# A hybrid mLSTM and DeltaNet block on one core: the order of the wide output blocks, the loads of the last stage, the values' factors, and the queue of the heads' turned outputs

## The chip, the cores and the metric

The kernel runs on one core of one Trainium2 chip. The metric is the device time of one execution in microseconds, as the median of several runs; lower is better.

## The reference, cut to what matters

S = 512 tokens, D = 2048 channels, float32, one layer: RMSNorm, one input projection that is cut into two token mixers and their gates, and one output projection whose halves are merged by gates and added to the residual.

```python
u = _rmsnorm(h, norm_w)
proj = jnp.matmul(u, w_in)                # ml q,k,v,o,z,i,f; dn qkv,z,b,a; gate_a, gate_b
...
h_a = _mlstm_chunkwise(q, k, v, i_pre, logf)          # 8 heads, 128 / 256 wide
h_a = _merge_heads(_rmsnorm(h_a)) * ml_norm_w * sigmoid(ml_o) * silu(ml_z)
...
qkv = _causal_conv_silu(dn_qkv, dn_conv_w)            # 4 taps
h_b = _gated_delta_chunkwise(l2norm(q), l2norm(k), v, beta, g)   # 16 heads, 128 wide
h_b = _merge_heads(_rmsnorm(h_b) * dn_norm_w * silu(dn_z))
...
# delta rule, chunk by chunk, after a triangular solve for w_val and w_k:
u = wv - wk @ S;  o = qd @ S + qk_c @ u;  S_new = ge * S + ke.T @ u
...
y_a, y_b = h_a @ w_out[:ML_WIDTH], h_b @ w_out[ML_WIDTH:]
out = rmsnorm(h + sigmoid(gate_a) * y_a + sigmoid(gate_b) * y_b)
```

## The kernel before, in words

Each float32 operand of a large product is split into a high part (a cast on ACT, line 135, `wh`) and a low part (a subtraction on DVE, line 138, `wl`), and each product is three matmuls of 128 x 128 by 128 x 512: high by high, low by high, high by low.

The program has these stages. First RMSNorm and the first projections, to about 24 us and a little beyond. Then a long row of stages `seven`, which make the projections for gates and values with seven products instead of eight (to about 1062 us). Then the mixers (1062 to 1835 us): eight units `dn_unit`, each with two DeltaNet heads, amid the projections `proj_cm` of the next units (PE's lines 261 to 263, product `pj`) and the mLSTM heads. Then the output projection: three blocks of 512 columns by `wide_block` (blocks 0 and 1 for the mLSTM half, and block 2 over the DeltaNet half, 1940 to 1996 us), two stages `seven`, and a last block.

A unit of the mixers runs `dn_front_k` and `dn_front_q` and then `dn_back`, which inverts the triangular blocks of both heads in four steps (PE products `p1` to `p4`, with copies into `ta` and `tb` between them) and starts two chains `dn_chain`, one for each head. A chain's first product is `pw`, line 1006, which takes `tb` and the values `vn` (tile `vt`). The values must have been multiplied by the keys' norms `nk` (line 980). At its end a chain makes the squares' sums `ssq` (line 1034), and multiplies its accumulator `po` by the gate `gz` (line 1040): with that the accumulator's bank is free. `turn` then transposes the result on DVE (line 796, tile `to`), and `travel` sends it in four DMAs of 64 KB each to `h_d` in memory (line 806). mLSTM heads go to `hm_d` in the same way.

`wide_block` has four accumulators `ps`, one for 128 tokens each (chunk c), in banks of three pools: `psj` (that of the projections), `psw` (small work) and `pso` (the chains' accumulators). A step is one row block kt of the weights: for c = 0 to 3 three matmuls (lines 1315 to 1317), with a tick after c = 1 and after c = 3. The last KTAIL steps are done chunk by chunk, each followed by `put_y(c)` (line 1338). Blocks 0 and 1 start while the last unit still works; `close()` looks after every step whether pools can be given back, and with the last starts `h_last`.

Block 2 takes DeltaNet's hidden rows. `load_h2` loads 16 tiles `hr`, in turn from `he_d` and `h_d`, through four buffers, and splits each into `uh` and `ul` (line 1189). `he_d` holds half-sums that `h_sums` and, for the last two heads, `h_last` make (`hsum`, lines 1248 to 1251, scaled into `tu`) and write. `h_last` waits five ticks, then loads the last two heads into two of the same four buffers. `lead` prepares the stage after block 2: three `load_quad` of three loads each (line 505). The gates of block 2 are loaded into the tile X (line 1330).

The order of work: PE runs in the order in which the program is written. For the other engines a scheduler orders the instructions by simulated time and priority. `tick()` moves the program's clock by one step, once every six matmuls, and lets generators go on that were given to `start(gen, wait)`; `yield n` waits n ticks. `urgent(level)` raises the priority. `behind(e)` places an instruction on engine e's queue right behind the newest split or weight load there, instead of where its priority would take it. `newest["S"]` is the newest weight load on SyncE's queue (SP).

Of the kernel before, what the change touches and what calls it, by code (L numbers as in the profile page):

```python
# [55 lines left out]
def hybrid_body(  # L56
# [83 lines left out]
    def behind(eng):  # L140

        return tc.issue_after(newest[eng])
# [102 lines left out]
    psw = pss.enter_context(tc.tile_pool(name="psw", bufs=3, space=PSUM))  # L245
    pso = pss.enter_context(tc.tile_pool(name="pso", bufs=2, space=PSUM))

    banks = (((psj, "pj"),) * 3 + ((psw, "wk"),), ((psw, "wk"),) * 2 + ((pso, "o"),) * 2)

    def proj_cm(col0, before=None, kind="i"):  # L250
        ps = [psj.tile([P, S], F32, tag="pj", name="pj") for _ in range(2)]
# [232 lines left out]
    def seven_stage(sbp, su, s4, X, t2_d, w_, k0, blocks, sinks, hook):  # L484
# [5 lines left out]
                 for g in "AB" for i in range(KH)]  # L490
        rawq, partq = [], {}

        def load_quad():
            if len(rawq) == len(quads):
                return
            _, c1, c2, b, g, i = quads[len(rawq)]
            with tc.high_priority(offset=2 * PRIO):
                r = sbp.tile([P, 3, NO], F32, tag="wr3", name="wr3", bufs=3)
                k1, k2 = (slice((k0 + 2 * i + n) * P, (k0 + 2 * i + n + 1) * P) for n in range(2))
                if g == "A":  # L500
                    src = (w_[k1, c1:c1 + NO], w_[k1, c2:c2 + NO], w_[k2, c2:c2 + NO])
                else:
                    src = (w_[k2, c1:c1 + NO], w_[k2, c2:c2 + NO], t2_d[b % 2, i])
                for n in range(3):
                    nc.sync.dma_start(r[:, n, :], src[n])  # L505
            rawq.append(r)

        def split(src, wide):
            if wide:
# [92 lines left out]
                    hook()  # L602
                product(n, m)

        def lead():
            for _ in range(3):
                load_quad()
                yield 2
            prep_sums(0)
            prep_pair(0)  # L610
            yield 1
# [151 lines left out]
    def bc(col, n):  # L763
        return col.unsqueeze(2).to_broadcast([P, NC, n])

    def conv_silu(ps, ct, dst, level=1):
        yp = yps[cnt["yp"] % NYP]
        cnt["yp"] += 1
        with urgent(level):
            A.copy(yp[:, 3:S + 3], ps)  # L770
            A.mul(dst, yp[:, 3:S + 3], convc[:, 144 + ct:145 + ct])
# [27 lines left out]
    def travel(o, dst, out, apart):  # L799

        d = dst if len(dst.shape) == 4 else dr.tile([16, BS, 4, BS], F32, tag="td", name="td", bufs=8)
        ov = o.rearrange("p n (j c) -> p (n j) c", c=BS)
        if out:
            for a in range(4):
                with behind("A"):
                    nc.scalar.dma_start(d[:, :, a, :].rearrange("m r c -> r m c"), ov[a * BS:(a + 1) * BS])
# [124 lines left out]
    def dn_back(hs, kq, u):  # L931
# [15 lines left out]
        for q in range(2):  # L947
            a1 = slice(64 * q + 32, 64 * q + 64)
            with urgent():
                A.mul(s1[a1], p1[a1], -1.0)  # L950
        yield 2
        p2 = psw.tile([P, 2, 2 * NC, BS], F32, tag="wk", name="p2")
        for g, a in G2:
# [20 lines left out]
            T.matmul(p4[0:64, g, :], s3[64:128, g, :], tb[64:128, g, 64:128], start=True, stop=True)  # L974
        with urgent():
            V.tensor_copy(tb[0:64, :, 64:128], p4[0:64])
        for j in range(2):
            vn = u["vs"][j]
            with behind("V"):
                V.tensor_tensor(out=vn, in0=vn, in1=bc(u["nk"][:, j, :], P), op=ALU.mult)  # L980
        start(dn_chain(0, hs, kq, u), 2)
        start(dn_chain(1, hs, kq, u), 3)

    def dn_chain(j, hs, kq, u):
        h = hs[j]
# [57 lines left out]
    def dn_unit(p, mh):  # L1043
# [28 lines left out]
            start(load_h(), 2, "B")  # L1072
        ps = proj_cm(DN_Q + dcol)
        u["qn"] = []
        for j in range(2):
            conv_silu(ps[j], hs[j], kq[j][:, 1, :], 3 if last else 1)
            qn = wp.tile([P, NC, P], F32, tag="tg", name="qn", bufs=3)
            u["qn"].append(qn)
            start(silu_end(kq[j][:, 1, :], (kq[j][:, 1, :], qn)), 4 + 3 * j, front)
# [148 lines left out]

    def h_raw(i):
        if i == KH - 1:  # L1230
            raw = [late["sb"].tile([P, S], F32, tag="hs", name="hs", bufs=4) for _ in range(2)]
        elif i % 2:
            raw = [wk.tile([P, S], F32, tag="rb", name="hs", bufs=3) for _ in range(2)]
        else:
            pair = wk.tile([P, 2, S], F32, tag="ls", name="hs", bufs=1)
            raw = [pair[:, n, :] for n in range(2)]
        with behind("S"):
            for n in range(2):
                load_tile(raw[n], h_d[2 * i + n])
        return raw  # L1240
# [29 lines left out]

    def h_last():

        yield 5
        raw = h_raw(KH - 1)
        yield 5
        yield from h_pair(KH - 1, raw)
# [42 lines left out]
    def wide_w(col, kt):  # L1319
        return [w[:, 0, :] for w in next_w("o", col, kt)]  # L1320

    def wide_block(nb, pools, place, then=()):

        sl = slice(nb * NO, (nb + 1) * NO)
        ps = [pool.tile([P, NO], F32, tag=t, name="py") for pool, t in pools]
        tgs = {}

        def load_tg(c):
            tgs[c] = place(c)
            nc.sync.dma_start(tgs[c], tg_d[c, :, sl])  # L1330

        def load_tgs():
            for c in range(NC - (nb == 1)):
                load_tg(c)
            yield 1

        def put_y(c):
            V.scalar_tensor_tensor(out=tgs[c], in0=tgs[c], scalar=1.0, in1=ps[c], op0=ALU.add, op1=ALU.mult)
# [12 lines left out]
        for kt in ks[:KT - KTAIL]:  # L1351
            w = wide_w(nb * NO, kt)
            for c in range(NC):
                products(ps, kt, c, *w, ks)
                if c % 2:
                    tick()
            if nb < YDRAIN:
                close()
        ws = [(kt, wide_w(nb * NO, kt)) for kt in ks[KT - KTAIL:]]
        for c in range(NC):  # L1360
            for kt, w in ws:
                products(ps, kt, c, *w, ks)
            tick()
            if c in tgs:
                with urgent(3):
                    put_y(c)
            else:
                start(put_last(), 1)
# [2 lines left out]
             wk.tile([P, NO], F32, tag="rb", name="tgy", bufs=3) if c == 2 else wp.tile([P, NO], F32, tag="tg", name="tgy", bufs=3),  # L1371
             lambda c: wp.tile([P, NO], F32, tag="tg", name="tgy", bufs=3))
    for b in range(YDRAIN):
        wide_block(b, ((psj, "pj"), (psw, "wk"), (psj, "pj"), (psj, "pj")), DRAIN[b])
    while "sb" not in late:
        tick()
        close()
# [278 lines left out]
```

## Time and profile before

| | |
|---|---|
| median of 3 runs | 2220.33 us (2218.37 to 2221.66) |
| the profiled execution | 2217.53 us |
| its span, first to last instruction | 2215.8 us |
| mean granted TensorE clock | 0.995 |
| mixers | 1062.7 to 1835.0 us |
| blocks 0 and 1 | 1835.0 to 1940.7 us |
| block 2 | 1940.7 to 1996 us |

How to read the lines below: a row of a timeline has the start in us, the duration, engine, line, operation, output <- inputs and the shape; in square brackets the idle time of the engine before it and what ended it. A row of the waits has the engine and line that waited, what ended the wait, the total in us, how often, and the longest. A row of the DMAs has the transfer, the queue that issued it, how many, KB each, and the median us from issue to landing. SPq is SyncE's queue, ACTq that of ScalarE.

### The profile page before, as it was taken

How to read it: one execution, taken by the hardware profiler on the slowest of the kernel's cores; microseconds unless marked ns; L12 is line 12 of the kernel's file. 1: busy time of each engine (PE TensorE's matmuls, PEld its weight loads, DVE VectorE, ACT ScalarE, POOL GpSimd, SP SyncE). 2: the span in 40 equal slices, each digit the busy share in tenths (PEclk: the TensorE clock that was granted, in tenths of full speed). 3: DMA queues.
4: the chain of work that ended last, by engine and by line, in shares of the span. 5: the costliest groups of instructions: out<-in, count | busy, mean ns of one | idle time of the engine just before them, and what ended most of it. 6: DMA issues, size and time to landing. Idle time of an engine off the chain costs nothing.

```text
span 2215.8 us, 31667 instructions
## 1 busy us (share of the span) xinstructions
PE 2156.6 (97%) x10592; PEld 1770.1 (80%) x10592; DVE 1655.4 (75%) x2883; ACT 1022.3 (46%) x1986; POOL 279.5 (13%) x388
## 2 busy tenths in 40 slices
PE   6999999999999999999999999999999999989997
PEld 5877778887878888888888888888888887867775
DVE  5787788788778777777587886757575777667875
ACT  5444444444444444444545545444545464334344
POOL 0320000000000000000223323213131211110101
PEclk9999999999999999999999999999999999999999
DMA  5455676667677766766677767667666668696896
GB/s 157 119 182 180 197 214 198 210 197 223 199 217 238 227 192 225 233 229 213 190 195 165 184 161 182 161 171 174 167 154 153 154 166 221 176 265 189 249 326 215
DMA packets 532774, 435.81 MB, mean 197 GB/s; under 512 B 241921, under 2 KB 393698, under 8 KB 532482
## 3 DMA queue, kind: packets, MB, share of 16 engines
q1 hardware_dynamic: 420450, 349.29, 55.3%
q10 hardware_dynamic: 105568, 68.77, 9.8%
q0 software_dynamic: 6592, 15.73, 3.7%
q8 instruction: 83, 1.36, 0.3%
q14 instruction: 81, 0.66, 0.1%
HBM read 342.37 MB, written 95.49 MB: 198 GB/s over the span
## 4 chain that ended last, share of the span: by engine, by line
PE 71%; DMA 12%; DVE 9%; issue 4%; ACT 2%; SPq 2%; POOL 1%; ACTq 0%; DVEq 0%; POOLq 0%
PE ps L576 10%; PE ps L577 10%; PE ps L575 10%; PE pj L261 9%; PE pj L263 9%; PE pj L262 9%; DVE wl L138 4%; DMA wr<-t_d 4%; DMA wr<-in_w_in_dram 2%; PE py L1315 2%; PE py L1316 2%; PE py L1317 2%; ACT wh L135 1%; SPq L505 1%; DVE X L617 1%
## 5 line engine op out<-in xcount | busy, mean ns | idle before, releaser
L135 ACT CAST wh<-wr 128x512 fp32r<-128x512 f32 (+1 forms) x538 | 379.6, 707 | 411.3 <-PE pj L262 225.0
L138 DVE TENSOR_TENSOR wl<-wr,wh 128x512 fp32r<-128x512 f32 (+1 forms) x538 | 440.9, 822 | 154.8 <-ACT wh L135 150.5
L261 PE MATMUL pj<-uh,wh 128*128 128x512 f32 x1024 | 427.2, 417 | 0.0
L263 PE MATMUL pj<-uh,wl 128*128 128x512 f32 x1024 | 401.1, 392 | 0.0
L262 PE MATMUL pj<-ul,wh 128*128 128x512 f32 x1024 | 400.5, 391 | 0.0
L576 PE MATMUL ps<-wl,uh 128*128 128x512 f32 x704 | 277.1, 394 | 7.4 <-DVE wl L138 7.2
L575 PE MATMUL ps<-wh,uh 128*128 128x512 f32 x704 | 276.1, 392 | 4.4 <-DVE X L617 3.9
L577 PE MATMUL ps<-wh,ul 128*128 128x512 f32 x704 | 274.3, 390 | 0.0
L135 ACT CAST wh<-ts 128x512 fp32r<-128x512 f32 x224 | 138.2, 617 | 256.0 <-DVE ts L535 200.2
L135 ACT CAST wh<-t 128x1024 fp32r<-128x1024 f32 x112 | 117.8, 1052 | 248.6 <-PE ps L577 133.1
L263 PEld LDWEIGHTS pj<-uh,wl 128*128 128x128 f32 x1024 | 192.5, 188 | 42.3
L576 PE MATMUL ps<-wl,suh 128*128 128x512 f32 x576 | 224.2, 389 | 1.7 <-DVE wl L138 1.7
L575 PE MATMUL ps<-wh,suh 128*128 128x512 f32 x576 | 224.3, 389 | 0.6 <-ACT qk L353 0.3
L577 PE MATMUL ps<-wh,sul 128*128 128x512 f32 x576 | 224.1, 389 | 0.0
L261 PEld LDWEIGHTS pj<-uh,wh 128*128 128x128 f32 x1024 | 193.4, 189 | 34.9
L262 PEld LDWEIGHTS pj<-ul,wh 128*128 128x128 f32 x1024 | 193.5, 189 | 32.9
L138 DVE TENSOR_TENSOR wl<-ts,wh 128x512 fp32r<-128x512 f32 x224 | 153.6, 689 | 38.6 <-ACT wh L135 38.6
L138 DVE TENSOR_TENSOR wl<-t,wh 128x1024 fp32r<-128x1024 f32 x112 | 137.7, 1229 | 48.3 <-ACT wh L135 47.6
L576 PEld LDWEIGHTS ps<-wl,uh 128*128 128x128 f32 x704 | 132.2, 188 | 44.1 <-DVE wl L138 18.3
L575 PEld LDWEIGHTS ps<-wh,uh 128*128 128x128 f32 x704 | 132.1, 188 | 39.2 <-DVE X L617 11.3
L535 DVE TENSOR_TENSOR ts<-wr 128x512 f32<-128x512 f32 x112 | 77.3, 690 | 102.0 <-DMA wr<-t_d 76.1
L577 PEld LDWEIGHTS ps<-wh,ul 128*128 128x128 f32 x704 | 132.2, 188 | 26.4
(305 smaller groups left out, 3499.8 us busy)
## 6 DMA issues: line engine op xcount, KB each, us to landing
wr<-in_w_in_dram SPq DMA_DIRECT2D x704, 256.0 KB, 3.7
wr<-in_w_out_dram SPq DMA_DIRECT2D x138, 256.0 KB, 5.0
t_d<-ts ACTq DMA_DIRECT2D x96, 256.0 KB, 4.2
wr<-t_d SPq DMA_DIRECT2D x96, 256.0 KB, 4.0
wr<-in_w_in_dram SPq DMA_DIRECT2D x64, 128.0 KB, 3.3
xt<-in_x_dram SPq DMA_DIRECT2D x8, 512.0 KB, 7.3
tg_d<-X ACTq DMA_DIRECT2D x16, 256.0 KB, 5.5
tg_d<-to ACTq DMA_DIRECT2D x16, 256.0 KB, 5.0
```

The costliest lines, as they stand in the source:

```text
L135: newest["A"] = A.copy(hi, src).ins
L138: newest["V"] = V.tensor_tensor(out=lo, in0=src, in1=hi.bitcast(F32), op=ALU.subtract).ins
L261: T.matmul(ps[j], hi[:, k, wsl], uh[:, kt, :], start=(kt == 0), stop=False)
L262: T.matmul(ps[j], hi[:, k, wsl], ul[:, kt, :], start=False, stop=False)
L263: T.matmul(ps[j], lo[:, k, wsl], uh[:, kt, :], start=False, stop=(kt == KT - 1))
L535: V.tensor_tensor(out=ts[:, 0, :], in0=r[:, 0, :], in1=r[:, 2, :], op=ALU.subtract)
L575: T.matmul(ps[t], ah, hi, start=(g == "A" and i == 0), stop=False, skip_group_check=True)
L576: T.matmul(ps[t], ah, lo, start=False, stop=False, skip_group_check=True)
L577: T.matmul(ps[t], al, hi, start=False, stop=(i == KH - 1), skip_group_check=True)
L1315: T.matmul(ps[c], uh[:, kt, tsl], hi, start=(kt == ks[0]), stop=False)
L1316: T.matmul(ps[c], uh[:, kt, tsl], lo, start=False, stop=False)
L1317: T.matmul(ps[c], ul[:, kt, tsl], hi, start=False, stop=(kt == ks[-1]))
```

## The change

It has six parts. Line numbers of the kernel after are 8 to 17 higher.

1. `wide_block` takes `behind_` and `ending`. In block 0 (`behind_` = 2) the first two steps are done for chunks 0 and 1, and then for chunks 2 and 3; in block 2 the last steps end in the order of chunks 2, 0, 1, 3. Block 2's banks are (psw, psw, pso, psj) instead of (psw, psw, pso, pso).
2. `lead` for the stage after block 2 issues its nine loads one a tick behind the newest weight load, starting at tick 14 instead of three quads at raised priority from tick 18.
3. In `dn_back` the multiplications of the values by the norms come after the first step instead of after the fourth, and the chains start one tick later.
4. `travel` issues the DMAs of `h_d` and `hm_d` from SP's queue, behind the newest weight load, instead of from ACT's.
5. In the last unit the copies of both heads' last projection (`conv_in`) are written ahead of the filters.
6. `h_last` loads into the tile X, which is still empty then, and without its first wait.

```diff
-    banks = (((psj, "pj"),) * 3 + ((psw, "wk"),), ((psw, "wk"),) * 2 + ((pso, "o"),) * 2)
+    JB, WB, OB = (psj, "pj"), (psw, "wk"), (pso, "o")
...
-        def lead():
+        def lead(apart=False):
             for _ in range(3):
-                load_quad()
-                yield 2
+                if apart:
+                    for to, src in quad_parts():
+                        with behind("S"):
+                            nc.sync.dma_start(to, src)
+                        yield 1
+                else:
+                    load_quad()
+                    yield 2
...
-    def conv_silu(ps, ct, dst, level=1):
+    def conv_in(ps, level=1):
         yp = yps[cnt["yp"] % NYP]
         cnt["yp"] += 1
         with urgent(level):
             A.copy(yp[:, 3:S + 3], ps)
+        return yp
...
-                with behind("A"):
-                    nc.scalar.dma_start(d[:, :, a, :].rearrange("m r c -> r m c"), ov[a * BS:(a + 1) * BS])
+                with behind("S"):
+                    nc.sync.dma_start(d[:, :, a, :].rearrange("m r c -> r m c"), ov[a * BS:(a + 1) * BS])
...
                 A.mul(s1[a1], p1[a1], -1.0)
+        for j in range(2):
+            vn = u["vs"][j]
+            with behind("V"):
+                V.tensor_tensor(out=vn, in0=vn, in1=bc(u["nk"][:, j, :], P), op=ALU.mult)
         yield 2
...
             V.tensor_copy(tb[0:64, :, 64:128], p4[0:64])
-        for j in range(2):
-            vn = u["vs"][j]
-            with behind("V"):
-                V.tensor_tensor(out=vn, in0=vn, in1=bc(u["nk"][:, j, :], P), op=ALU.mult)
-        start(dn_chain(0, hs, kq, u), 2)
-        start(dn_chain(1, hs, kq, u), 3)
+        start(dn_chain(0, hs, kq, u), 3)
+        start(dn_chain(1, hs, kq, u), 4)
...
+        yq = [conv_in(ps[j], 3) for j in range(2)] if last else (None, None)
         for j in range(2):
-            conv_silu(ps[j], hs[j], kq[j][:, 1, :], 3 if last else 1)
+            conv_silu(ps[j], hs[j], kq[j][:, 1, :], yp=yq[j])
...
         if i == KH - 1:
-            raw = [late["sb"].tile([P, S], F32, tag="hs", name="hs", bufs=4) for _ in range(2)]
+            raw = [late["X"][:, 0, n, :] for n in range(2)]
...
     def h_last():
 
-        yield 5
         raw = h_raw(KH - 1)
...
-        for kt in ks[:KT - KTAIL]:
-            w = wide_w(nb * NO, kt)
-            for c in range(NC):
-                products(ps, kt, c, *w, ks)
-                if c % 2:
-                    tick()
-            if nb < YDRAIN:
+        ws = {}
+        order = [(kt, c) for c in (0, 2) for kt in range(behind_) ] + [(kt, c) for kt in ks[behind_:KT - KTAIL] for c in (0, 2)]
+        for n, (kt, c0) in enumerate(order):
+            if c0 == 0:
+                ws[kt] = wide_w(nb * NO, kt)
+            for c in (c0, c0 + 1):
+                products(ps, kt, c, *ws[kt], ks)
+            tick()
+            if n % 2 and nb < YDRAIN:
                 close()
         ws = [(kt, wide_w(nb * NO, kt)) for kt in ks[KT - KTAIL:]]
-        for c in range(NC):
+        for c in ending:
...
-        wide_block(b, ((psj, "pj"), (psw, "wk"), (psj, "pj"), (psj, "pj")), DRAIN[b])
+        wide_block(b, (JB, WB, JB, JB), DRAIN[b], behind_=0 if b else 2)
...
-    wide_block(YDRAIN, banks[1], lambda c: X2[:, c // 2, c % 2, :], [(load_h2(), 1), (lead(), 18)])
+    wide_block(YDRAIN, (WB, WB, OB, JB), lambda c: X2[:, c // 2, c % 2, :], [(load_h2(), 1), (lead(True), 14)], ending=(2, 0, 1, 3))
```

Three places show how the instructions move. On ACT at the start of block 0, where the last unit's copies of a projection (`yp` <- `pj`) free two of the block's banks, there stands before (`kq` are the filters' outputs, `hr` the hidden rows of the mLSTM half):

```order
L1189 ACTIVATE uh<-hr,normc 128x512 x2
L135 CAST wh<-wr 128x512
L806 DMA h_d<-to 32x16x32 x3
L770 COPY yp_9097<-pj 128x512
L806 DMA h_d<-to 32x16x32
L771 ACTIVATE kq_17041<-yp_9097,convc 128x512
L770 COPY yp_9099<-pj 128x512
L135 CAST wh<-wr 128x512
L806 DMA h_d<-to 32x16x32 x2
L771 ACTIVATE kq_17042<-yp_9099,convc 128x512
```

and after:

```order
L135 CAST wh<-wr 128x512
L1205 ACTIVATE uh<-hr,normc 128x512
L779 COPY yp_9097<-pj 128x512
L1205 ACTIVATE uh<-hr,normc 128x512
L786 ACTIVATE kq_17041<-yp_9097,convc 128x512
L135 CAST wh<-wr 128x512
L1205 ACTIVATE uh<-hr,normc 128x512
L779 COPY yp_9099<-pj 128x512
L786 ACTIVATE kq_17042<-yp_9099,convc 128x512
```

The six issues of `h_d` have left ACT's row, and two scalings of hidden rows and a cast now stand between the two copies, where one multiplication stood.

On DVE at the end of block 1 and the head of block 2, where the last unit's two chains end (`gz` <- `po` frees a chain's bank), there stands before:

```order
L1034 SCALAR_TENSOR_TENSOR ssq<-ssq,qe 128x4
L1040 TENSOR_TENSOR gz<-po,gz 128x512
L1338 SCALAR_TENSOR_TENSOR tgy<-tgy,py 128x512
L796 STREAM_TRANSPOSE to<-gz 128x512
L1338 SCALAR_TENSOR_TENSOR tgy<-tgy,py 128x512
L138 TENSOR_TENSOR wl<-wr,wh 128x512
L1248 TENSOR_TENSOR hsum<-hs 128x256
L1250 TENSOR_TENSOR hsum<-hs 128x256
L1190 SCALAR_TENSOR_TENSOR tu<-hsum,normc,tu 128x768
L1040 TENSOR_TENSOR gz<-po,gz 128x512
```

and after:

```order
L1049 SCALAR_TENSOR_TENSOR ssq<-ssq,qe 128x4 x2
L1353 SCALAR_TENSOR_TENSOR tgy<-tgy,py 128x512 x2
L138 TENSOR_TENSOR wl<-wr,wh 128x512
L1264 TENSOR_TENSOR hsum<-hs 128x256
L1266 TENSOR_TENSOR hsum<-hs 128x256
L138 TENSOR_TENSOR wl<-wr,wh 128x512
L1265 TENSOR_TENSOR hsum<-hsum,hs 128x256
L1206 SCALAR_TENSOR_TENSOR tu<-hsum,normc,tu 128x768
L1055 TENSOR_TENSOR gz<-po,gz 128x512
```

The first chain's multiplication has moved behind the second's sum of squares, two outputs of block 1, two weight splits, three sums and a scaling; the second chain's follows two rows below.

On SP, the queue of loads in block 2, the last gates of block 1 (`tgy`) are followed before by:

```order
L1330 DMA tgy<-tg_d 128x512
L176 DMA wr<-in_w_out_dram 128x512 x4
L505 DMA wr_19285<-in_w_out_dram 128x512 x3
L176 DMA wr<-in_w_out_dram 128x512
L505 DMA wr_19311<-in_w_out_dram 128x512 x3
L505 DMA wr_19337<-in_w_out_dram 128x512
L176 DMA wr<-in_w_out_dram 128x512
L505 DMA wr_19337<-in_w_out_dram 128x512 x2
L1289 DMA hr<-he_d 128x512
L1186 DMA hr<-h_d 128x4x128
```

and after by:

```order
L1345 DMA tgy<-tg_d 128x512
L176 DMA wr<-in_w_out_dram 128x512 x2
L821 DMA h_d<-to 32x16x32 x5
L176 DMA wr<-in_w_out_dram 128x512
L821 DMA h_d<-to 32x16x32 x3
L1202 DMA X_19056<-h_d 128x4x128
L176 DMA wr<-in_w_out_dram 128x512
L1202 DMA X_19056<-h_d 128x4x128
L1304 DMA hr<-he_d 128x512
L1202 DMA hr<-h_d 128x4x128
```

The nine loads of the last stage (`wr_...`, line 505) no longer stand ahead of the first hidden rows `hr`; the two heads' outputs and the loads of them into X stand there instead, with weight loads between and behind them.

In `dn_back` the two multiplications (line 980, now 969) stood before the copy into `tb` (line 976) in DVE's row, two rows ahead in most units; after, they stand 11 to 23 rows ahead of it (line 995).

More of the change, by code (lines that the diff above doesn't have):

```diff
@@ L491, in seven_stage, with quad_parts @@
         rawq, partq = [], {}
+        def quad_parts():
+            _, c1, c2, b, g, i = quads[len(rawq)]
+            r = sbp.tile([P, 3, NO], F32, tag="wr3", name="wr3", bufs=3)
+            k1, k2 = (slice((k0 + 2 * i + n) * P, (k0 + 2 * i + n + 1) * P) for n in range(2))
+            if g == "A":
+                src = (w_[k1, c1:c1 + NO], w_[k1, c2:c2 + NO], w_[k2, c2:c2 + NO])
+            else:
+                src = (w_[k2, c1:c1 + NO], w_[k2, c2:c2 + NO], t2_d[b % 2, i])
+            rawq.append(r)
+            return [(r[:, n, :], src[n]) for n in range(3)]
         def load_quad():
@@ L495, in load_quad @@
                 return
-            _, c1, c2, b, g, i = quads[len(rawq)]
             with tc.high_priority(offset=2 * PRIO):
[L498 to L506, printed above, removed]
+                for to, src in quad_parts():
+                    nc.sync.dma_start(to, src)
         def split(src, wide):
@@ L603, in seven @@
                 product(n, m)
-        def lead():
+        def lead(apart=False):
             for _ in range(3):
-                load_quad()
-                yield 2
+                if apart:
+                    for to, src in quad_parts():
+                        with behind("S"):
+                            nc.sync.dma_start(to, src)
+                        yield 1
+                else:
+                    load_quad()
+                    yield 2
             prep_sums(0)
@@ L770, in conv_silu @@
             A.copy(yp[:, 3:S + 3], ps)
+        return yp
+    def conv_silu(ps, ct, dst, level=1, yp=None):
+        if yp is None:
+            yp = conv_in(ps, level)
+        with urgent(level):
             A.mul(dst, yp[:, 3:S + 3], convc[:, 144 + ct:145 + ct])
@@ L1320, in wide_w, with wide_block @@
         return [w[:, 0, :] for w in next_w("o", col, kt)]
-    def wide_block(nb, pools, place, then=()):
+    def wide_block(nb, pools, place, then=(), behind_=0, ending=range(NC)):
         sl = slice(nb * NO, (nb + 1) * NO)
```

## The prediction

> **What bounds the kernel now.** I read the page's busy times first, then the waits of TensorE (PE) over the whole run, then PE's timeline at those of them that the change touches, with the granted clock behind each.
>
> ```profile
> PE 2156.6 (97%) x10592; PEld 1770.1 (80%) x10592; DVE 1655.4 (75%) x2883; ACT 1022.3 (46%) x1986; POOL 279.5 (13%) x388
> PE pw L1006 <- DVE tb L976: 4.0, 4, 1.9
> PE py L1315 <- ACT wh L135: 5.9, 3, 4.1
> PE py L1315 <- ACT yp L770: 2.1, 2, 1.8
> PE py L1315 <- DVE gz L1040: 1.9, 1, 1.9
> PE ps L575 <- DVE X L1338: 1.6, 1, 1.6
> ```
>
> TensorE is busy for 97% of 2215.8 us, and the change removes none of its matmuls. So only two things can be gained: its idle time, and matmuls run at less than the full clock. In the rows of the waits the columns are the total in us, the times and the longest. The five rows touch lines that the change moves: 4.0 + 5.9 + 2.1 + 1.9 + 1.6 = 15.5 us. Where they stand:
>
> ```profile
> 1676.95 0.49 PE L1006 MATMUL pw<-vt,tb 128*128 128x128 f32 x2 [1.90 <-DVE tb L976]
> 1838.31 0.50 PE L1315 MATMUL py<-wh,uh 128*128 128x512 f32 x1 [1.77 <-ACT yp L770]
> 1942.12 0.39 PE L1315 MATMUL py<-wh,uh 128*128 128x512 f32 x1
> 1942.57 0.39 PE L1317 MATMUL py<-wh,ul 128*128 128x512 f32 x1
> 1944.87 0.47 PE L1315 MATMUL py<-wh,uh 128*128 128x512 f32 x1 [1.92 <-DVE gz L1040]
> 1988.46 0.80 PE L1315 MATMUL py<-wh,uh 128*128 128x512 f32 x1 [4.14 <-ACT wh L135]
> 1998.37 0.50 PE L575 MATMUL ps<-wh,tu 128*128 128x512 f32 x1 [1.60 <-DVE X L1338]
> ```
>
> Behind some of them the clock falls. The columns of the windows are busy time by engine, then PEclk, the granted clock:
>
> ```profile
> 1677.00:1680.40 3.40, 3.40 (x18) 2.88 (x19) 3.40 (x6) 2.65 (x12) 0.00 (x0) 1.00 0.28 73
> 1839.82:1843.23 3.41, 3.41 (x9) 2.64 (x10) 3.41 (x9) 2.86 (x6) 0.00 (x0) 0.50 1.20 311
> 1945.64:1949.04 3.40, 3.40 (x9) 2.64 (x8) 2.48 (x5) 0.90 (x2) 0.00 (x0) 0.50 0.99 221
> 1988.46:1993.42 4.96, 4.87 (x11) 3.50 (x12) 3.79 (x7) 2.17 (x3) 0.60 (x1) 0.50 0.80 249
> ```
>
> At clock 0.50 half of the stretch is lost: 3.41 / 2 = 1.7 us after block 0's wait, 1.7 us at the head of block 2, 4.96 / 2 = 2.5 us at its end. After the wait of 1.90 us in the mixers nothing is lost (1.00). Of the row of 5.9 I count only the longest wait, 4.1. So the ceiling of the gain is 4.0 + (2.1 + 1.7) + (1.9 + 1.7) + (4.1 + 2.5) + 1.6 = 19.6 us.
>
> The Trainium skill's "TensorE: Matmul & The Clock Gate", section "What's actually happening", lets the array fall to half rate after an idle window of about 3.4 us. The trace differs: 1.77 and 1.92 us of idling were enough at two places, and 1.90 us at a third was not. By the rule only the 4.14 us wait would carry a clock loss, and the ceiling would be lower by 3.4 us; the rows decide.
>
> **The change part by part.** All durations are from the profiled execution: 2217.53 us, 2215.8 of span and 1.7 around it, against a median of 2220.33. A saving is taken off either alike.
>
> *The values' factors (dn_back).* In DVE's timeline two multiplications by the norms stand ahead of the copy for which `pw` waits:
>
> ```profile
> 1673.57 1.29 DVE L980 TENSOR_TENSOR vt<-vt,nk 128x512 f32<-128x512 f32 x2
> 1676.22 0.68 DVE L976 COPY tb<-p 64x512 f32<-64x512 f32 x1
> ```
>
> The copy comes 1.29 us sooner without them, and the chains start one tick later, six matmuls at (1942.57 − 1942.12) / 2 = 0.23 us, 1.4 us. Together 2.7 us of room against a longest wait of 1.90: all four go, **−4.0** (0 if the filters' operations in line 773 take the place; no more than −4.0, as the clock shows no loss here). The multiplications themselves now stand among filter work three program steps sooner; DVE is busy for 75%, and the steps between wait two or three ticks each, 2.7 to 4.1 us, so 1.3 us there is hidden. Should that cover be gone, the four waits come back one step sooner.
>
> *Block 0's order and the last unit's copies.* Chunks 2 and 3 of block 0 need banks that ACT's copies of the last projection free.
>
> ```profile
> 1837.67 0.59 ACT L770 COPY yp<-pj 128x512 f32<-128x512 f32 x1 [0.94 <-DVE wl L138]
> 1838.40 0.72 ACT L771 ACTIVATE kq<-yp,convc 128x512 f32<-128x512 f32 x1
> 1839.03 0.56 ACT L770 COPY yp<-pj 128x512 f32<-128x512 f32 x1
> 1839.49 0.62 ACT L135 CAST wh<-wr 128x512 fp32r<-128x512 f32 x1
> ```
>
> Now: 2.1 of idling and 1.7 of clock, 3.8 us. After, chunk 2 is wanted six matmuls (1.4 us) later, and ACT has no outputs to issue, whose place was in the 0.94 us of idling. But as the instructions stand now, two scalings of hidden rows, a multiplication and a cast lie between the two copies: 0.59 + 0.72 × 3 + 0.62 = 3.4 us from copy to copy, where it was 1839.03 − 1837.67 = 1.36 us. Copy 1 would end near 1837.67 + 3.4 + 0.56 = 1841.6, less the 0.94; chunk 3 is wanted at 1838.31 − 1.77 + 1.4 + 0.7 = 1838.6. That is about 2 us of waiting again: **0** (−3.8 if the scalings' loads come late and the copies pass first; +2 if the 0.94 isn't saved and the clock falls longer).
>
> *Block 2's banks.* Its chunk 3 waited for chain 1's accumulator, read by L1040; now chunk 3 has a bank that has long been free, and chunk 2 has chain 0's.
>
> ```profile
> 1943.12 1.00 DVE L1190 SCALAR_TENSOR_TENSOR tu<-hsum,normc,tu 128x768 fp32r<-128x768 f32 x1
> 1944.05 0.68 DVE L1040 TENSOR_TENSOR gz<-po,gz 128x512 f32<-128x512 f32 x1
> ```
>
> Before, chain 0's reader stood well ahead of this; in the new order on DVE it is behind both norms' sums, two more outputs of block 1, two weight splits, three sums and this `tu`, where chain 1's stood. So it ends near 1944.05 + 0.68 = 1944.7, while chunk 2 is wanted at 1942.12 (the row of PE above): 2.6 us instead of 1.92, and the same clock loss. **+0.5** (−3.6 if chain 0 stays ahead; +2.5 if the chain's later tick and the larger gap add up).
>
> *Block 2's end.* Its last weight cast came late because ACT takes it behind scalings that wait for loads, and SP had issued nine loads for the final stage ahead of those:
>
> ```profile
> 1957.68 1.28 SPq L505 DMA_DIRECT2D wr<-in_w_out_dram  x3
> 1964.20 0.33 SPq L1289 DMA_DIRECT2D hr<-he_d  x1
> 1987.18 0.72 ACT L1189 ACTIVATE uh<-hr,normc 128x512 fp32r<-128x512 f32 x1 [0.88 <-DMA hr<-h_d]
> 1987.81 0.60 ACT L135 CAST wh<-wr 128x512 fp32r<-128x512 f32 x1
> ```
>
> Now 4.14 + 2.5 = 6.6 us. After, the first loads of hidden rows pass the nine, which come one a tick, and h_last's two tiles take none of the four buffers those use. A new chain stands in SP's queue instead. L1040 of chain 1 ends near 1946; the transposes end near 1947.5; the issues and landings:
>
> ```profile
> L806 ACTq DMA_DIRECT2D h_d<-to x64: 309/443/2421, 1242.8 to 1951.8; - x64
> DMA to landing us min/median/max: 2.4/3.9/8.3
> hs<-h_d SPq DMA_DIRECT2D x2, 256.0 KB, 6.1
> he_d<-hs ACTq DMA_DIRECT2D x2, 256.0 KB, 5.0
> wr<-in_w_out_dram SPq DMA_DIRECT2D x19, 256.0 KB, 5.7
> X<-tg_d SPq DMA_DIRECT2D x4, 256.0 KB, 5.7
> ```
>
> Four issues of 0.44 make 1949.3, landing 3.9 makes 1953.2, the load of them 6.1 (1959.3), sums and scaling an estimated 3.5 (1962.8; the scaling alone is the 1.00 of `tu`), the sum written 5.0 (1967.8), and only then may X take its gates; a weight load behind their issues leaves at about 1969.2. Block 2 starts at 1940.7 (six matmuls ahead of 1942.12) and a step is 12 × 0.23 = 2.76 us, so its twelfth is used at 1940.7 + 11 × 2.76 + 3.6 (head) = 1974.7, and its load must leave at 1974.7 − 5.7 − 0.6 (cast) − 0.7 (split, an estimate from the cast) = 1967.7: 1.5 us late. So I keep 1.5 of the 6.6: **−5.1** (−6.6 to +3; more in the third rival).
>
> *The order of its end.* With chunk 2 and chunk 0 first, the final stage's first banks are read early: **−1.6** (to 0).
>
> *The outputs' queue.* 128 issues leave ACT for SP. In the mixers:
>
> ```profile
> SPq L176 <- DVE wl L138: 128.0, 69, 6.1
> td<-ke SPq DMA_DIRECT2D x8, 64.0 KB, 2.4
> wr<-in_w_in_dram SPq DMA_DIRECT2D x2, 256.0 KB, 2.8
> wr<-in_w_in_dram SPq DMA_DIRECT2D x186, 256.0 KB, 3.0
> L261 PE MATMUL pj<-uh,wh 128*128 128x512 f32 x1024 | 427.2, 417 | 0.0
> ```
>
> SP waits 128 us there for weight buffers to come free, so it is early; a head's four issues, 4 × 0.44 = 1.8 us, fit into that. A weight load issued amid 64 KB pieces (the third row, in a window of 9 us with eight such pieces) landed in 2.8 us against 3.0 for all 186, and no projection waits for its weights (0.0 in the last row). I take 0 in the mixers and **+0.7** for block 2, where outputs stand ahead of weights (0 to +6).
>
> The Trainium skill's "DMA: Bandwidth & Descriptors", section "Issuing engines are not separate DMA queues", says that issuing from several engines saves only the sequencer's time of starting the DMA. By it the 1.8 us a head would be the whole price; no run so far shows the outputs on SP.
>
> Sum: −4.0 + 0 + 0.5 − 5.1 − 1.6 + 0.7 = −9.5. The profiled execution would become 2208.0, the median 2210.8: **2211**. A measurement of this kernel can tell about 0.2%, 4.4 us, from no change.
>
> **The rivals.**
>
> *All of it goes.* The copies pass the scalings, chain 0 stays early, X's chain lands in time: −19.6, 2201. For it: each wait has one releaser, and each is moved. Against it: the new order on ACT and on DVE puts work between at two places.
>
> *Waits are replaced.* Only the factors' 4.0 goes; in the last stages each wait gets a successor of its size, since ACT, DVE and SP there still serve casts, scalings and loads in one order: −4, 2216. For it: DMA engines are 80 to 120% occupied in those windows (the number after PEclk, 0.80 to 1.20, a mean share), so loads that pass others make those late.
>
> *SP stands (slower).* In block 2 SP's queue now holds three landings in a row, outputs to X, X's half-sum out, gates into X, and weight loads stand behind each. By medians that costs 1.5 us. The landings to and from the outputs' tile reach from 2.4 to 8.3 us. If each of the three takes about 9 us instead of 3.9, 6.1 and 5.0, the weight load leaves 27 − 15 = 12 us later, 13.5 late in all; PE idles so long and then runs about 6 us at half clock, 3 more. Block 2's end is then 16.5 − 6.6 = +9.9 instead of −5.1, and the sum −9.5 + 15 = +5.5: 2226. Before and after come out even where the three landings take some 6.5 us longer in all: then the end costs 8 + 3 − 6.6 = +4.4, what the other terms save.
>
> **How the numbers follow.** Forecast 0.52, all goes 0.10, replaced 0.20, SP stands 0.18. The forecast's own bounds from the terms that are least known (0 ± 3 for each block's head, −5.1 ± 3) give 2206 to 2216. The range reaches to 2202 on the side of the first rival and to 2221 into the third; half of the first (0.05) and about 0.13 of the third are outside. Faster by over 0.2%: 0.50 + 0.10 + half of the second, 0.10 = 0.70. Within: 0.02 + 0.10 + 0.04 = 0.16. Slower: 0.14.
>
> **What would show it.** In the waits of PE the row of `pw` behind `tb` should be gone; a row of `p3` or `p4` in its place would show the multiplications hit another step. At block 0's head I expect one wait of about 2 us for the copy into `yp`, at block 2's head one of 2 to 3 for `gz`, each with a clock of 0.50 behind; at block 2's end under 2 us for `wh`. The row of `ps` behind `X` of the last outputs should be gone. L261 should wait under 2 us in all: more would show that outputs delay weights in the mixers, and prove the zero there wrong. An SP queue that stands over 10 us in block 2 for `h_d` or `he_d`, with a PE wait over 8 us, would be the third rival.

## The result and the profile after

The changed kernel is slower: 2226.51 us in the median of 9 runs (2222.05 to 2229.77) against 2219.61 of before (9 runs, 2217.31 to 2222.36), a ratio of 1.0026 with a 95% interval of 1.0015 to 1.0038. The forecast was 2211, so its direction was wrong.

The waits of TensorE in the changed kernel, in the columns of before (total in us, times, longest):

```profile
PE py L1330 <- DVE gz L1055: 5.3, 1, 5.3
PE py L1330 <- ACT wh L135: 5.3, 5, 3.3
PE pr L1013 <- DVE st L1032: 5.0, 2, 4.4
PE py L1330 <- ACT yp L779: 3.2, 2, 2.5
PE py L1331 <- DVE wl L138: 2.9, 6, 0.9
```

The waits of `pw` behind `tb` are gone, as forecast. But `pr`, the chains' next product, now waits 5.0 us for the state `st`, block 2's head waits 5.3 us for `gz` instead of 1.9, block 0's for `yp` 3.2 instead of 2.1, and the end of block 2 3.3 instead of 4.1. By stages, the first row of each pair the mixers and the second blocks 0 to 2 (busy time by engine, then PEclk, DMA share, GB/s); before:

```profile
1062.70:1835.02 772.32, 768.02 (x4414) 642.55 (x4412) 558.81 (x1373) 382.93 (x1001) 203.98 (x288) 1.00 0.70 171
1835.02:1995.93 160.91, 152.27 (x773) 123.72 (x772) 107.21 (x212) 62.01 (x127) 18.98 (x23) 0.96 0.78 220
```

and after:

```profile
1060.44:1836.65 776.21, 770.29 (x4413) 644.88 (x4412) 560.55 (x1372) 385.10 (x1001) 211.75 (x288) 1.00 0.71 170
1836.65:2006.13 169.48, 154.03 (x773) 124.14 (x772) 110.58 (x215) 64.69 (x131) 19.52 (x24) 0.96 0.78 215
```

The mixers lose 3.9 us: PE's idle time, stage less busy time, goes from 4.3 to 5.9, and its busy time grows by 2.3 for the same matmuls; an estimated 1.7 of that are the 3.5 us at clock 0.50 shown below. Blocks 0 to 2 lose 8.6: idle from 8.6 to 15.4, busy time 1.8 more. Ahead of the mixers this profile is 2.3 us shorter than that of before, and behind the blocks 1.3. The stages ahead of the mixers, which the change doesn't reach, differ by up to 8 us between the profiles of the kernels below, so stages of single profiles show where time goes, and the medians of the runs how much.

**Where the mixers lose.** In DVE's timeline the wait is one of 9 us for the loads `ls`, with the copy of the state behind it on the same engine:

```profile
1379.91 0.19 DVE L904 TENSOR_TENSOR tmp<-ls,xi 128x31 f32<-128x31 f32 x1 [8.96 <-DMA ls<-ld]
1380.69 0.28 DVE L1032 COPY st<-pst 128x128 f32<-128x128 f32 x1
```

TensorE's row there, and the granted clock behind:

```profile
1381.03 0.58 PE L1013 MATMUL pr<-st,kq 128*128 128x128 f32 x1 [4.39 <-DVE st L1032]
1381.00:1384.50 3.50, 3.47 (x10) 2.99 (x11) 3.26 (x14) 0.00 (x0) 0.00 (x0) 0.50 0.28 77
```

The `ls` are the triangles of the next unit, which the substitution on DVE (L904, L906) solves. SP's queue shows why they are late:

```profile
1369.50 2.31 SPq L827 DMA_DIRECT2D td<-kw  x4
1371.92 1.53 SPq L893 DMA_DIRECT2D ls<-ld  x2
1373.50 0.43 SPq L176 DMA_DIRECT2D wr<-in_w_in_dram  x1
1374.62 0.38 SPq L830 DMA_DIRECT2D kw<-td  x1
1375.05 0.96 SPq L893 DMA_DIRECT2D ls<-ld  x2
```

The mLSTM head's turned keys (`kw`, five transfers) and a weight load stand ahead of or between the four loads of `ls`, and the last leaves at 1375.6.

**Where block 2 loses.** DVE at the head of block 2:

```profile
1943.71 2.28 DVE L138 TENSOR_TENSOR wl<-wr,wh 128x512 fp32r<-128x512 f32 x1 [0.65 <-ACT wh L135]
1945.91 1.50 DVE L1264 TENSOR_TENSOR hsum<-hs 128x256 f32<-128x256 f32 x1
...
1947.68 0.68 DVE L138 TENSOR_TENSOR wl<-wr,wh 128x512 fp32r<-128x512 f32 x1
...
1948.61 1.01 DVE L1206 SCALAR_TENSOR_TENSOR tu<-hsum,normc,tu 128x768 fp32r<-128x768 f32 x1
1949.54 0.68 DVE L1055 TENSOR_TENSOR gz<-po,gz 128x512 f32<-128x512 f32 x1
```

The reader of chain 0's bank is at the place that the order showed, but the rows ahead of it take 5.8 us from 1943.7 on; TensorE wanted the bank at about 1945.1.

### The profile page after: what moved, and what is told of

Its sections match the earlier page's. It is cut to its first block, busy times and chain, and to the rows that moved or that the text cites. A ratio compares the mean times of both kernels' runs of the same rounds, so it can differ in the third digit from the quotient of the medians.

```text
span 2224.7 us, 31693 instructions
## 1 busy us (share of the span) xinstructions
PE 2159.2 (97%) x10592; PEld 1771.8 (80%) x10592; DVE 1657.4 (74%) x2883; ACT 1024.5 (46%) x1986; POOL 287.7 (13%) x388
```

## The experiments

Each ratio is to the kernel before, run beside it on the same chip, with its 95% interval. The runs stand on three chips, so a comparison of two of them by their ratios takes it that a ratio holds on each. "Mixers" and "blocks" are the stages above in that kernel's profile (before 772.3 and 160.9, changed 776.2 and 169.5). My theory at the start was that the outputs on SP's queue cost the mixers their time.

**1. Outputs back to ACT.** The changed kernel with

```diff
-                with behind("S"):
-                    nc.sync.dma_start(d[:, :, a, :]...
+                with behind("A"):
+                    nc.scalar.dma_start(d[:, :, a, :]...
```

> The changed kernel with one part undone: the heads' turned outputs are issued from ACT's queue again. Queue theory (outputs in SP's order delay the round trips ld and ls that the substitution on DVE waits for, and the loads of block 2): the mixers fall from 776.2 to about 768 us, the wait of pr for st (4.4 and 0.6 us) and its half clock go, and the whole falls by 6 to 10 us to 2217 to 2220 us. Order theory (the factors' new place and the chains' later tick put the chain's copies behind the substitution): the wait of pr stays, and the whole stays within 2 us of 2226.5.

1.0002 (0.9990 to 1.0013); mixers 771.3, blocks 162.4, and the longest wait of `pr` 0.6 us. Taken alone this would agree with the queue theory for the most part. But the wait for `gz` is 5.3 us, as in the changed kernel.

**2. Outputs to SP alone.** The kernel before with the reverse of that edit.

> The kernel before with one part of the change: the outputs issued from SP's queue behind weight loads. Queue theory: DVE waits for ls<-ld by 9 us or so at one or two places, PE waits for st, the mixers grow by 4 to 8 us, and the whole goes to 2224 to 2228 us. Order theory: within 2 us of before (2219.6), the mixers at 772 us.

0.9960 (0.9944 to 0.9976): faster, against both theories. Mixers 767.7, blocks 160.1. The outputs on SP's queue are no loss by themselves: alone, the move is worth 0.4%. That they cost something beside the factors' new place, as run 1 has it, stands all the same; runs 5 and 6 come back to it. ACT's waits of before in the mixers that end with an output's landing:

```profile
ACT tb L963 <- DMA hm_d<-to: 6.3, 2, 4.1
ACT wh L135 <- DMA h_d<-to: 4.2, 2, 2.1
ACT wh L135 <- DMA hm_d<-to: 4.0, 1, 4.0
```

No such row is left with the outputs on SP, and of the waits of `pw` one of 0.5 us:

```profile
PE pw L1006 <- DVE tb L976: 0.5, 1, 0.5
```

DVE's order around the copy of `tb` is the same there as before. So those waits came at least in part from the outputs in ACT's queue, not from the multiplications alone. A row of ACT's waits names what ended last, not what ACT needed: whether ACT stood for landings, or lost the time in which it issued the 128 transfers, these rows don't tell, and no run separates the two.

**3. Factors and chains alone.** The kernel before with part 3 of the change.

> The kernel before with one part of the change: the values' factors after dn_back's first step and the chains one tick later. Queue theory: the four waits of pw (4.0 us) go and nothing takes their place in the mixers, 2215.5 us; at the head of block 2 the chains' later end may give back 1 to 3 us. Order theory: pr waits 4 us or more for st, the whole is 2220 to 2224 us.

1.0032 (1.0022 to 1.0043). Slower, and by more than either theory had; mixers 771.5, with no row of `pr` among PE's waits, against the order theory, but blocks 170.0, with the same 5.3 us for `gz`.

**4. Factors and chains back.** The changed kernel without part 3.

> The changed kernel with one part undone: the values' factors after the fourth step and the chains one tick earlier, as before. Queue theory: the waits of pw (4.0 us) come back and DVE's wait for ls<-ld stays, so 2228 to 2231 us, unless the chains' earlier end shortens the wait at the head of block 2 by 2 to 3 us. Order theory: the wait of pr goes, 2218 to 2222 us.

0.9954 (0.9937 to 0.9971): 0.7% below the changed kernel and below both expectations. Mixers 767.7, blocks 157.5, the wait for `gz` gone. Without part 3 the loss is gone, and part 3 alone (run 3) makes one.

**5 and 6. Its two halves.** The changed kernel with the chains' start put back (5), or the multiplications (6):

```diff
-        start(dn_chain(0, hs, kq, u), 3)
-        start(dn_chain(1, hs, kq, u), 4)
+        start(dn_chain(0, hs, kq, u), 2)
+        start(dn_chain(1, hs, kq, u), 3)
```

> The changed kernel with only the chains' start put back (2 and 3 ticks); the factors stay after the first step. Chain theory (the tick by which the chains start later makes the last chain end later, and block 2 waits 5.3 us for it): the wait for gz falls to 1.5 us or less, blocks 0 to 2 take 157 to 162 us instead of 169.5, the whole falls by 6 to 10 us against the changed kernel, 0.3 to 0.5% below before. Factors theory (the multiplications in their new place push DVE's queue back): the wait for gz stays over 4 us and the whole within 3 us of the changed kernel, 0.1 to 0.4% above before.

> The changed kernel with only the factors put back after the fourth step; the chains keep their later start (3 and 4 ticks). Chain theory: the wait for gz stays at 4 to 5.5 us, blocks 0 to 2 take 167 us or more, the whole is 0.1 to 0.3% above before. Factors theory: it falls to the time of the kernel with both undone, 0.3 to 0.5% below before.

Chains back: 0.9990 (0.9980 to 1.0001), blocks 156.8, no wait for `gz`, mixers still 775.3. Factors back: 1.0003 (0.9992 to 1.0015), blocks still 168.7, mixers 769.5. Each theory is right for one stage and neither for the whole. Each half has its own place: in the profiles the chains' tick costs the blocks 11 to 13 us (runs 4 to 6 and the changed kernel), the factors' place the mixers 7 to 8; by the ratios the tick costs 0.36 to 0.49% and the factors' place 0.23 to 0.36%. Of the 12.7 us that the blocks of the changed kernel take more than those of run 5, 7.0 are idle time of PE and 5.7 busy time, at a mean clock of 0.96 instead of 0.98. The changed kernel with the chains back:

```profile
PE pr L1013 <- DVE st L1032: 3.9, 1, 3.9
```

and with the factors back:

```profile
PE py L1330 <- DVE gz L1055: 5.3, 1, 5.3
```

In the profiles the factors' place costs the mixers time only beside the outputs on SP's queue. With the factors moved and the outputs on ACT's queue (runs 1 and 3) the mixers take 771.3 and 771.5 us; with the outputs on SP's queue and the factors as before (runs 2, 4 and 6), 767.7 to 769.5; with both moved (the changed kernel and run 5), 776.2 and 775.3 us. In run 1 the turned keys stand ahead of and between the triangles as well:

```profile
1362.13 2.26 SPq L827 DMA_DIRECT2D td<-kw  x4
1364.50 1.36 SPq L893 DMA_DIRECT2D ls<-ld  x3
1366.28 0.38 SPq L830 DMA_DIRECT2D kw<-td  x1
1366.71 0.50 SPq L176 DMA_DIRECT2D wr<-in_w_in_dram  x1
1367.26 0.46 SPq L893 DMA_DIRECT2D ls<-ld  x1
```

But without outputs in that queue its last load of triangles is issued 312.2 us after the mixers' start, and 315.6 us in the changed kernel.

**7 and 8. Outputs issued twice,** on ACT's queue in the kernel before (7) and on SP's in the kernel of run 2 (8), with a tile `d2` that nobody reads:

```diff
+            d2 = dr.tile([16, BS, 4, BS], F32, tag="dd", name="d2", bufs=8)
...
+                    nc.scalar.dma_start(d2[:, :, a, :]...
```

> The kernel before, with each of the outputs' DMAs issued twice on ACT's queue, the second into a tile that nobody reads. Standing theory (ACT stands at such issues until earlier transfers have landed, and its copies and casts behind them come late): ACT's waits ended by DMAs in the mixers grow, the waits of pw too, and the whole grows by 4 us or more (0.2%). Traffic theory (only the bytes and the landings count): as much as the double on SyncE's queue.

> The kernel before with the outputs on SyncE's queue, each DMA issued twice there, the second into a tile that nobody reads. Standing theory: SyncE is early in the mixers, so the second issues cost under 2 us against the outputs once on SyncE's queue: 0.3% below before. Traffic theory: 4 us or more above that, near before.

1.0055 (1.0040 to 1.0070) on ACT, 0.55% above the kernel it doubles; 1.0015 (1.0004 to 1.0025) on SP, also 0.55% above its own (0.9960). In the profiles the mixers are 786.5 and 776.8 us. Against the standing theory: by the ratios the second set costs the same on either queue, and far from under 2 us. A second set is dear wherever it is issued; why the first is cheaper on SP rests on run 2 and ACT's waits there, not on this pair.

**10 and 11. The triangles first.** In the changed kernel (10), and in that of run 5 (11):

```diff
         for q in range(4):
-            nc.sync.dma_start(ls[q * NSYS:(q + 1) * NSYS], ...
+            with urgent(3):
+                nc.sync.dma_start(ls[q * NSYS:(q + 1) * NSYS], ...
```

> The changed kernel with one thing more: the four loads ls of the substitution's triangles get a higher priority on SyncE's queue, so that the turned keys (td<-kw) and a weight load no longer stand between them. Order-on-SyncE theory (the factors' and chains' new places let the scheduler put those ahead of the last ls; DVE stands 9 us for it with a chain's copy of st behind, PE 4.4 us): DVE's longest wait for ls<-ld falls under 4 us, the wait of pr for st under 1 us, the mixers fall from 776 to 768 to 771 us, the blocks stay at 167 to 170 us, and the whole is 0.0 to 0.1% below before. Factors theory (DVE itself is late through the multiplications): the wait of pr stays at 3 us or more and the whole 0.2% above before.

> The changed kernel with the chains' start put back and the ls loads first; the factors stay after the first step. Order-on-SyncE theory: the factors' new place costs nothing of its own, the mixers take 767 to 769 us, blocks 0 to 2 156 to 159 us, and the whole is 0.4 to 0.5% below before, as with both undone. Factors theory: the mixers stay over 773 us, 0.1% below before.

1.0005 (0.9993 to 1.0018) and 0.9953 (0.9938 to 0.9968); mixers 770.4 and 769.3, blocks 166.6 and 155.7. DVE's waits for the triangles in the changed kernel, in run 10 and in run 11:

```profile
DVE tmp L904 <- DMA ls<-ld: 13.6, 4, 9.0
```

```profile
DVE tmp L905 <- DMA ls<-ld: 6.1, 2, 4.3
```

```profile
DVE tmp L905 <- DMA ls<-ld: 3.7, 2, 2.6
```

With the loads first and the factors still in their new place the 4.4 us wait is gone: the longest for `st` is 1.1 us in run 10 and 0.2 in run 11. So the multiplications cost nothing that can be measured on DVE itself: run 11 has them in their new place and run 14 below, on the same chip, in their old one, both with the triangles first, and the ratios are 0.9953 and 0.9958. What their place cost came by the order that the scheduler then gave to SP's queue. (Run 10's longest wait for `ls`, 4.3, is a little above the 4 us expected.)

**12. The nine loads.** Run 4 with `lead()` as before.

> The changed kernel with factors and chains put back, and the nine loads for the stage after block 2 as before as well (three at raised priority from tick 18). If those nine loads' place sets the wait at the end of block 2: the last wait for wh is 2 us or more longer than the 4.9 us with the loads one a tick, and the whole 0.1 to 0.3% higher. If block 2's transfers as a whole set it: the wait stays within 1.5 us of 4.9 and the whole within 0.1%.

0.9949 (0.9934 to 0.9964), the same as with the loads one a tick. The end of block 2 waits less, which neither theory had:

```profile
PE py L1330 <- ACT wh L135: 2.3, 3, 1.1
```

Blocks take 156.0 instead of 157.5, and what follows 223.2 instead of 219.9. Where the nine loads stand moves the waits of the last stages about, and no gain in the whole can be measured.

**14. Triangles first in run 4.**

> The changed kernel with factors and chains put back, and the ls loads first. Here DVE's longest wait for ls<-ld is 2.5 us already and no chain waits for it, so both theories give no more than 0.1% from the version without: 0.4 to 0.5% below before.

0.9958 (0.9943 to 0.9972): no difference from run 4 that the intervals show, as both theories had it.

**15. Last unit's chains back.** The changed kernel with

```diff
-        start(dn_chain(0, hs, kq, u), 3)
-        start(dn_chain(1, hs, kq, u), 4)
+        first = 2 if hs[0] == 2 * UNITS[-1][0] else 3
+        start(dn_chain(0, hs, kq, u), first)
+        start(dn_chain(1, hs, kq, u), first + 1)
```

> The changed kernel with the chains' start put back in the last unit alone; the other seven units keep 3 and 4 ticks. If the cost at the head of block 2 is the last unit's tick: the wait for gz falls from 5.3 to under 1.5 us, blocks 0 to 2 from 169.5 to 155 to 161 us, the mixers stay at 774 to 777 us with the wait of pr, and the whole is 0.0 to 0.15% below before. If it comes of the whole run of later chains: the blocks stay over 165 us.

1.0005 (0.9991 to 1.0019), not below before as expected; the wait for `gz` is gone, blocks 162.5, a little over the range, mixers 775.4. One tick of one unit sets the 5.3 us. The blocks don't come down to the 156.8 of run 5: block 0 waits 4.6 us for `yp` here, 1.9 there.

**9. The rest alone.** The changed kernel with outputs, factors and chains as before.

> The changed kernel with three parts undone: outputs on ACT's queue, factors and chains as before. What is left is the order of the blocks, block 2's banks and end, the loads one a tick, the copies and h_last. If the outputs' queue is worth its 0.4% beside these as it is alone: this is 0.0 to 0.15% below before, the mixers at 771 to 773 us with the waits of pw. If these parts already hold the gain: 0.3% or more below before.

0.9977 (0.9963 to 0.9991), between the two expectations; mixers 771.1 with 2.1 us of waits of `pw`, blocks 157.4. Blocks' order, banks, loads, copies and `h_last` together are worth about 0.2%, and the outputs' move beside them (run 4) about as much again.

**16. Both causes away at their places.** Run 15 with the triangles first.

> The changed kernel with the ls loads first and the last unit's chains put back: the two causes that the runs so far point to, each taken away at its own place, the factors and seven units' chains left as changed. If these two are the whole loss: mixers 768 to 771 us, blocks 155 to 160 us, 0.35 to 0.5% below before. If the chains' tick costs more in the mixers: 0.2% or less below before.

0.9975 (0.9963 to 0.9986), between the two expectations; mixers 771.3, blocks 159.5. That is half a per cent below the changed kernel, but not the 0.47% below before of run 11, which differs by the tick of the other seven units: their tick costs about 0.2% more, some 2 us in the mixers and 4 in the blocks of these profiles, there mostly `yp` at block 0 (2.9 us against 0.8). So the two causes, each taken away at its own place, are not the whole loss; the tick of all eight units and the triangles' order are: with both taken away (run 11) the ratio is that of run 4.

The versions of runs 4, 11 and 12 beat both kernels, by 0.46 to 0.51% against before; their intervals overlap, so none is the best. That of run 2 (0.9960) overlaps with them too: the outputs' move alone gives most of what these versions gain.

## Why the prediction was wrong, step by step

**The factors and the chains' tick (−4.0): the step that failed.** The four waits went, but "all four go" with "the clock shows no loss here" left out what the moves do to other queues: the path to `pr` over DVE's copy of `st`, the substitution and the triangles' loads on SP had no term. In the changed kernel, `pr` and `pst` wait 5.9 us instead, and 3.5 us behind 1381.0 ran at clock 0.50. Run 10 shows the carrier: with the triangles first on SP, 776.2 becomes 770.4. The bound "0 if the filters' operations in line 773 take the place" looked at DVE alone. So the mixers took 3.9 us more by the profile, where 4.0 less were forecast. And the gain was counted, at least in part, for the wrong change: the outputs' move alone leaves only 0.5 of the 4.0 us (run 2).

**Block 2's banks (+0.5): right in kind, mis-sized.** (From 1.92 to 2.6 is +0.7, not +0.5.) The chunk waited behind the rows that I named. I put the end of chain 0's reader where chain 1's had stood, which gave a wait of 2.6 us. It was 5.3, 2.7 more, since the chains' tick moved the reader behind a stretch of DVE work that was itself stretched. I had counted that tick as room in the mixers and in block 2 only as an upper bound. Runs 5 and 15 show that this tick alone makes it.

**Block 0 (0):** a wait of about 2 us for the second copy was forecast; it was 2.5 with 0.8 ahead of it, 3.2 in all against 2.1, with about the same loss of clock (3.25 us at 0.53). The tick has a part in it: run 5, which differs by it alone, has 1.9. But run 1, with the tick, has 1.9 as well, and run 4, without it, 0.8; what else sets this wait is not shown.

**Block 2's end (−5.1): failed.** The wait fell only from 4.1 to 3.3, and two more followed, where before there was none:

```profile
1988.69 0.50 PE L1330 MATMUL py<-wh,uh 128*128 128x512 f32 x1 [3.34 <-ACT wh L135]
1998.41 0.49 PE L1330 MATMUL py<-wh,uh 128*128 128x512 f32 x1 [0.99 <-ACT wh L135]
1999.84 0.50 PE L1331 MATMUL py<-wl,uh 128*128 128x512 f32 x1 [0.94 <-DVE wl L138]
```

The gates for X left SP at 1967.5, near the 1967.8 that I had counted, and the first hidden rows at 1963.8. The load for which ACT stood the longest left late, behind three of the nine loads for the stage after, which now come one a tick:

```profile
1979.33 2.27 SPq L613 DMA_DIRECT2D wr<-in_w_out_dram  x3
1981.69 0.53 SPq L1304 DMA_DIRECT2D hr<-he_d  x1
1987.41 0.72 ACT L1205 ACTIVATE uh<-hr,normc 128x512 fp32r<-128x512 f32 x1 [4.64 <-DMA hr<-he_d]
```

ACT still stands here for hidden rows, with the cast behind it. (That it is this load is my reading from the time of its landing.) Run 12 shows that moving the nine loads, to which I had put the old wait down, is not what it takes: with them as before the wait is 1.1 us at most, where run 4, with them one a tick, has 4.9. What sets this end remains open, since the two runs take the same time in all.

**The order of its end (−1.6):** the row of `ps` behind `X` of the last outputs is gone, as forecast.

**The outputs' queue (0 in the mixers, +0.7): the zero failed both ways.** SP was early, as I had read, and no projection waited for its weights in the changed kernel, as forecast. But the outputs were in ACT's way: alone the move takes 4.6 us from the mixers' profile and 0.40% from the time (run 2). Beside the factors' new place it adds 4.9 us to the mixers (771.3 in run 1, 776.2 in the changed kernel), and with the triangles first these are 770.4 (run 10). The +0.7 for block 2 can't be told from nothing: in run 2 the blocks take 160.1 us, before 160.9. The Trainium skill's "DMA: Bandwidth & Descriptors", section "Issuing engines are not separate DMA queues", counts only the sequencer's time for starting a DMA. The runs don't contradict it: a second set costs 0.55% on either queue (runs 7 and 8), and by the medians of line 806 in the kernel before, 0.310 us for the 64 issues to `hm_d` and 0.443 for the 64 to `h_d`, issuing took an estimated 48 us of ACT's queue, more than the move gained.

**The rivals.** "Waits are replaced" described most of it: in the last stages the waits had successors, in sum larger ones (PE's idle time there went from 8.6 to 15.4 us). But it let the factors' 4.0 us go, and these were replaced as well. The slower rival had the sign but not the mechanism: the outputs in SP's queue in block 2 were not what made it slower, since run 4 keeps them there and is 0.46% faster than before. Its sign, SP standing over 10 us there, did not show either: SP's longest wait for `h_d` in block 2 was 4.3 us.

## What to carry to other kernels

Where a scheduler orders the queues by simulated time, moving one operation on one engine also reorders the transfers of others: compare every in-order queue that feeds a waiting engine, above all for small loads that stand between larger ones. A start that is one tick later is not free room but a shift of all that hangs on it, and it is dearest where the last user of a bank meets its next owner. An engine with a low share of busy time (ACT at 46%) can still be late: look at what stands in its queue before the engine whose instruction comes last is blamed. And a change of several parts is worth running part by part: here one part alone was worth 0.4%, and together with another it was a loss.

## What was not expected of the hardware

At block 2's head the same split of 128 x 512 took 2.28 us on DVE where the next took 0.68, while POOL ran products on the gates:

```profile
1943.90 1.32 POOL L1052 TENSOR_TENSOR gz<-gz,rsd 128x512 f32<-128x512 f32 x1
1945.50 1.62 POOL L1052 TENSOR_TENSOR gz<-gz,rsd 128x512 f32<-128x512 f32 x1
```

The two long rows of DVE (from 1943.71 and 1945.91) lie across these. The Trainium skill's "SBUF — State Buffer", section "SBUF: two separate sides", says that an operation of DVE with two inputs in SBUF and one of POOL that reads SBUF lock each other out for a whole instruction, whichever starts first. The rows agree in kind, though DVE's split starts 0.19 us ahead of POOL's product and is still the one stretched, and no run took POOL's product away. In the mixers of the changed kernel 14 of 224 such splits took over 1 us, up to 2.63, and each of the 14 lies across an instruction of POOL; others that do so stayed at 0.7 to 0.9.

The wait for `gz` itself is 5.3 us in all five kernels whose last unit has the later chains (changed, runs 1, 3, 6 and 10), on either queue of the outputs and with either set of banks: the transfers around it don't move it.
